# Two-layer hybrid decoder trunk in split float32: buffers of weight parts, rounds of the down projection, and the way of the 32x32 blocks

## The chip, the cores and the metric

The kernel runs on one core of one Trainium2 chip. The metric is the device time of one execution in microseconds (us), lower is better. Before the change three runs gave 2683.37, 2684.74 and 2685.12 us; the median is 2684.74 us. A further execution was profiled: it took 2684.28 us, of which the profile's span covers 2682.6 us.

## What is computed

Input x is 256 tokens by 2048 channels in float32. Two layers follow each other; each is, cut to what matters:

```
h = rms_norm(x); q, k, v, uv, gates = split(h @ w_in)         # 2048 -> 7680
a = sliding_window_attention(rope(norm(q)), rope(norm(k)), v, sinks) @ w_attn_branch
b = chunked_sgu(gelu(uv)) @ w_sgu_branch
x = x + (sigmoid(gates_a) * a + sigmoid(gates_b) * b) @ w_out  # 2048 -> 2048
h2 = rms_norm(x)
x = x + (silu(h2 @ w_gate) * (h2 @ w_up)) @ w_down             # 2048 -> 5632 -> 2048
```

All weights are float32 in HBM, some 235 MB a layer, and each is read once.

## The kernel before

**Three products for one.** A float32 product is made from three matmuls in a rounded 32-bit format: every weight tile is split into a high part `whi` (ScalarE, L199) and the remainder `wlo` (VectorE, L200), every activation unit into `uh` and `ul`; `add_product` (L274 to L283) adds uh by whi, uh by wlo and ul by whi for two blocks of 128 rows. Activations are the stationary operand (128 x 128), weights the moving one (128 x 512).

**Entries.** The work of TensorE is one list of entries. An entry is one weight tile of 256 rows by 512 columns (a raw tile, 512 KB): tags X, G and U stand for a tile that is multiplied with both token blocks (12 matmuls of 512 columns). `single` makes a product of one column chunk. `pair` handles two column chunks (gate and up of the feed-forward, or two chunks of w_out or w_down) and computes the first 512 rows of them by a seven-product scheme in place of eight: tags P1, P2, P6, P7, P4, P5, P3, each 6 matmuls. These need sums of raw tiles (`sums`, L192 on VectorE), taken in place in four tiles k11, k12, k21, k22 that have one buffer each. P6 reads k11 after k12 := k22 - k12 and k11 := k11 + k12; P4 and P5 each need one more sum. After P1, P6 and P7 ScalarE copies a PSUM bank away (`snap`, L307); after P5 VectorE adds one bank to a copy (L309).

**Order.** The body of a pair is G, P5, G, P3, then G and U entries. Where one product ends and a pair begins, the last four entries of the former (t0 to t3 below) are woven between the pair's head: t0, P1, P2, t1, P6, t2, P7, t3, P4. In `pair` a constant TAIL = 6 says how many U entries stand at the end; for w_down, whose pairs have 8 or 10 G and U entries each, the earlier ones alternate.

**Stream.** At every step `Stream.next` asks for loads up to W_LOAD = 5 entries from the current one, splits up to W_SPLIT = 3 entries, the sums of an entry standing right before its split, and hands out the parts. So at the step of entry n the parts of entry n + 2 are issued. There are 3 buffers of `hi` and of `lo` (pool `wsp`), 4 of raw tiles (`wraw`, tag raw) and 28 slots of 4 KB a partition (`big`) for activations. All loads are issued from the SP queue, which is in order.

**Steps.** Other work is put off with `after(n, fn)`: it is run n ticks later, a tick being one entry of 12 matmuls or two of 6. Within an engine this work is placed behind the split that was issued last (`issue_after`). The order of TensorE is that of the program; on the other engines a planner at build time sets the order.

**Turning.** Activations that were computed as tokens by channels must be turned before they can be a stationary operand. `turn` (L342) transposes 32x32 blocks on VectorE into `box` (L349), the second token block a tick later, and 16 small DMAs of 32 KB (L353, SP queue) carry the blocks to the right partitions in `tt` within the next ticks. `transposed` then makes `uh` and `ul` (6 and 7 ticks after the call; for the chunk that the seven-product scheme uses 6 to 9 ticks). With `on_pe` TensorE transposes instead (L391).

**Feed-forward.** `hidden` computes one chunk of 512 of the 5632 hidden channels (eleven in all); the down projection runs in two rounds, after chunks 0 to 4 and after 5 to 10 (ROUNDS). Each round takes two pairs (columns in four chunks) and adds its result to x (`residual`, L805).

Of the kernel before, what the change touches and what calls it, by code (L numbers as in the profile page):

```python
# [8 lines left out]
F32 = mybir.dt.float32  # L9
F32R = mybir.dt.float32r  # L10
AF = mybir.ActivationFunctionType
ALU = mybir.AluOpType
AX = mybir.AxisListType

P = 128
NT = 2
# [11 lines left out]
CW = 512  # L28
NCH = D // CW
EPS = 1e-6  # L30
B = 32
W_LOAD = 5
ROUNDS = ((0, 5), (5, 11))
WINO = 0
TAIL = 6
W_SPLIT = 3
N_WARM = 8
TT = 1
K_TURN = 7
# [11 lines left out]
def hybrid_trunk(ctx: ExitStack, tc: tile.TileContext, x, mix_norm, w_in, q_norm, k_norm, sinks,  # L51
# [3 lines left out]

    const = ctx.enter_context(tc.tile_pool(name="const", bufs=1))
    lay = ctx.enter_context(tc.tile_pool(name="lay", bufs=1))
    big = ctx.enter_context(tc.tile_pool(name="big", bufs=28))
    wraw = ctx.enter_context(tc.tile_pool(name="wraw", bufs=4))
    wsp = ctx.enter_context(tc.tile_pool(name="wsp", bufs=3))  # L60
    tmp = ctx.enter_context(tc.tile_pool(name="tmp", bufs=5))
    turned = ctx.enter_context(tc.tile_pool(name="turned", bufs=TT))
    small = ctx.enter_context(tc.tile_pool(name="small", bufs=4))
    ps_acc = ctx.enter_context(tc.tile_pool(name="ps_acc", bufs=4, space=bass.MemoryType.PSUM))
# [5 lines left out]
    def nm(s):  # L70
        names[0] += 1
        return f"{s}_{names[0]}"
# [41 lines left out]

        return Plan(key, [], [half(w, h, "X") for h in range(w.shape[0] // (2 * P))])

    def pair(key, wa, wb):

        h1, h2 = 2 * WINO, 2 * WINO + 1
        l11, l12, l21, l22 = (load_of(w, h, t) for w, h, t in ((wa, h1, "k11"), (wb, h1, "k12"), (wa, h2, "k21"),
                                                              (wb, h2, "k22")))
        k11, k12, k21, k22 = l11[0], l12[0], l21[0], l22[0]
        rest = [h for h in range(wa.shape[0] // (2 * P)) if h // 2 != WINO]
        g, u = [half(wa, h, "G") for h in rest], [half(wb, h, "U") for h in rest]
        head = [dict(tag="P1", loads=[l11], src=k11), dict(tag="P2", loads=[l21], src=k21),
                dict(tag="P6", loads=[l12, l22], sums=[(k12, k22, "-", k12), (k11, k11, "+", k12)], src=k11),
                dict(tag="P7", loads=[], src=k12), dict(tag="P4", loads=[], sums=[(k21, k21, "-", k11)], src=k21)]
        p5 = dict(tag="P5", loads=[], sums=[(k11, k22, "-", k11)], src=k11)  # L130
        p3 = dict(tag="P3", loads=[], src=k22)
        body = [g[0], p5, g[1], p3]
        n_mid = len(u) - TAIL
        for i, e in enumerate(g[2:]):
            body.append(e)
            if i < n_mid:
                body.append(u[i])
        body += u[min(n_mid, len(g) - 2):]
        return Plan(key, head, body)

    plans = []
    for l in range(DEPTH):
        wl = w_in[l]
        for kind, c in FIRST_PART:
            o = {"kv": O_KV, "q": 0, "v": O_V, "u": O_U, "gate": O_GATE}[kind] + c * CW
            plans.append(single(("in", l), wl[:, o:o + CW]))
        plans += [single(("att", l), w) for w in cols_of(w_attn_branch[l], NCH)]
        for j in range(NCH):
            plans.append(single(("in", l), wl[:, O_GATE + D + j * CW:O_GATE + D + (j + 1) * CW]))
            plans.append(single(("sgu", l), w_sgu_branch[l, :, j * CW:(j + 1) * CW]))  # L150
        c_ = cols_of(w_out[l], NCH)
        plans += [pair(("mix", l), c_[j], c_[j + 1]) for j in range(0, NCH, 2)]
        for r, (f0, f1) in enumerate(ROUNDS):
            for f in range(f0, f1):
                plans.append(pair(("ffn", l), w_gate[l, :, f * CW:(f + 1) * CW], w_up[l, :, f * CW:(f + 1) * CW]))
            c_ = cols_of(w_down[l, f0 * CW:f1 * CW, :], NCH)
            plans += [pair(("hid", l, r), c_[j], c_[j + 1]) for j in range(0, NCH, 2)]
    entries = []
    for p in plans:
        if p.head:  # L160
# [5 lines left out]
    class Stream:  # L166
# [2 lines left out]

        def __init__(self):  # L170
            self.raws, self.parts = {}, []
            self.asked = self.at = 0

        def load(self, upto):
            while self.asked < min(upto, len(entries)):
# [8 lines left out]
                    self.raws[key] = raw  # L184
                self.asked += 1

        def split(self, upto):
            while len(self.parts) < min(upto, len(entries)):
                e = entries[len(self.parts)]
                for d, x, op, y in e.get("sums", ()):  # L190
                    with tc.issue_after(self.last.ins):
                        self.last = nc.vector.tensor_tensor(out=self.raws[d], in0=self.raws[x], in1=self.raws[y],  # L192
                                                            op=ALU.add if op == "+" else ALU.subtract)
                raw = self.raws[e["src"]]
                hi = wsp.tile([P, 2, CW], F32R, tag="hi", name=nm("whi"))
                lo = wsp.tile([P, 2, CW], F32R, tag="lo", name=nm("wlo"))
                one = len(self.parts) < 2
                for i in ([slice(0, 1), slice(1, 2)] if one else [slice(0, 2)]):
                    nc.scalar.activation(hi[:, i, :], raw[:, i, :], AF.Copy)  # L199
                    self.last = nc.vector.tensor_tensor(out=lo[:, i, :], in0=raw[:, i, :], in1=hi[:, i, :].bitcast(F32),  # L200
                                            op=ALU.subtract)
                self.parts.append((hi, lo))

        def next(self):
            self.load(self.at + W_LOAD)
            self.split(self.at + W_SPLIT)
            self.at += 1
            return self.parts[self.at - 1]

# [6 lines left out]
    def after(n, fn):  # L216
        steps.append((slot_no[0] + n, fn))
# [41 lines left out]

    units_at = {}  # L260
    turn_of = [0]
    debt = [0]

    def block(units, h, t):

# [2 lines left out]

    def banks(p, which):
        if which not in p.acc:  # L270
            p.acc[which] = [ps_acc.tile([P, CW], F32, tag="acc", name=nm("acc")) for _ in range(NT)]
        return p.acc[which]

    def add_product(p, ps, u, w):  # L274
# [64 lines left out]
        while p.left:  # L339
            step()  # L340

    def turn(dst, src, per=1):  # L342


        box = turned.tile([P, 4, 4, NT, B], F32, tag="box", name=nm("box"))
        iv = src.rearrange("p t (k j c) -> p t k j c", j=4, c=B)

        def blocks(t):
            nc.vector.transpose(box[:, :, :, t, :].rearrange("p j k r -> p k j r"), iv[:, t])  # L349

        def move(j):
            for i in range(4):
                nc.sync.dma_start(dst[j * B:(j + 1) * B, i], box[i * B:(i + 1) * B, j])  # L353

        blocks(0)
        after(1, lambda: blocks(1))
        for j in range(4):
            after(1 + j // per, lambda j=j: move(j))

    def transposed(units, c, src, cols=None, on_pe=False, wino=False):  # L360

# [37 lines left out]
        def blocks_of(k0):  # L399
            return lambda k, step: tt[:, :, k0 + k:k0 + k + step].rearrange("p i k t r -> p (k t) i r")  # L400

        if not wino:
            def done():
                parts(2, 2, blocks_of(2))
                units[c] = (uh, ul)

            after(6, lambda: parts(0, 2, blocks_of(0)))
            after(7, done)
            return

        flat = {}
# [24 lines left out]
            split_(sh, sl, flat["s"])  # L436
            units[c] = (uh, ul, sh, sl)

        after(6, lambda: scaled(0))
        after(7, lambda: scaled(2))  # L440
        after(8, sums)
        after(9, finished)

    class Norm:

# [144 lines left out]
    class Attention:  # L590
# [46 lines left out]
        def keys(self, kv):  # L637
            self.kv = kv
            kd = slot([P, NT, NKV, 2, HD], name="kd")
            self.rotate(kv[:, :, :KVW], NKV, self.pl.rope[1], [kd[:, :, :, j, :] for j in range(2)])  # L640
            self.kT = slot([P, 4, NKV, NT, B], name="kT")
            after(K_TURN, lambda: turn(self.kT, kd.rearrange("p t n a d -> p t (n a d)"), 2))

        def queries(self, c, q):
            self.rotate(q, NQ // 2, self.pl.rope[0], None)
# [10 lines left out]
        def turn_queries(self, c, q):  # L656
            tt = slot([P, 4, 4, NT, B], name="tt")

            def ordered(k):
                nc.scalar.activation(self.qT[c][:, k:k + 2].rearrange("p k (t i r) -> p (k t) i r", t=NT, r=B),  # L660
                                     tt[:, :, k:k + 2].rearrange("p i k t r -> p (k t) i r"), AF.Copy)

            turn(tt, q, 2)
            after(4, lambda: ordered(0))
            after(5, lambda: ordered(2))

# [155 lines left out]
    for l in range(DEPTH):  # L822
# [44 lines left out]
        if l + 1 < DEPTH:  # L867
            after(20, lambda: prepare(l + 1))

        def hidden(hT, c, wino):  # L870
            hid = slot([P, NT, CW], name="hid")

            def added(sums):
# [12 lines left out]
            def on_up(sums):  # L886
                up = added(sums)
                for t in range(NT):
                    nc.vector.scalar_tensor_tensor(out=hid[:, t, :], in0=up[t], scalar=norm.rr[t], in1=hid[:, t, :],  # L889
                                                   op0=ALU.mult, op1=ALU.mult)  # L890
                after(2, lambda: transposed(hT, c, hid, wino=wino))

            product_pair(("ffn", l), on_gate, on_up)

        for r, (f0, f1) in enumerate(ROUNDS):
            hT = units_at["hid", l, r] = [None] * (f1 - f0)
            for f in range(f0, f1):
                hidden(hT, f - f0, f - f0 == WINO)
            if f1 < NF:
                residual(("hid", l, r))  # L900
            elif l + 1 < DEPTH:
# [42 lines left out]
```

## Time and profile before

| | |
|---|---|
| median of 3 runs | 2684.74 us (2683.37 to 2685.12) |
| profiled execution | 2684.28 us, span 2682.6 us |
| full matmuls (512 columns) | 3 x 3516 |
| DMA traffic | 506.20 MB, mean 189 GB/s |
| w_out, w_gate, w_up, w_down loads | 64, 176, 176, 176 of 512 KB |

Times are us unless marked ns. PE is TensorE's matmul, PEld its weight load, DVE VectorE, ACT ScalarE, POOL GpSimd, SP the queue that issues the DMAs. Matmuls are pipelined: the recorded duration of one is longer than the distance to the next. In the rows of waits, "who <- whom: total, times, longest" is the idle time of an engine before an instruction and what ended it. In groups of instructions the number after x is the count, then busy us and mean ns of one, then the idle time before them.

### The profile page before, as it was taken

Reading aid. Unit: us, or ns where it says so; the run is one execution under the profiler, and the core shown is the slowest. Engines: PE = TensorE matmul, PEld = TensorE weight load, DVE = VectorE, ACT = ScalarE, POOL = GpSimd, SP = SyncE. Lnnn points to the kernel's source line nnn. Section 1 sums busy time; section 2 is a strip of 40 time slices with the busy share of each in tenths; the row PEclk is TensorE's granted clock in tenths of the full one; section 3 lists DMA queues with packets and bytes.
Section 4 is the critical chain, followed back from the end, with each engine's and each line's share of the span. In section 5 each row is a group of like instructions: output and inputs, shape, how many; then the busy total and the mean of one; then the engine's idle time right before and its main releaser. Section 6 shows DMA issues by size and latency. Waiting matters only on the chain.

```text
span 2682.6 us, 30911 instructions
## 1 busy us (share of the span) xinstructions
PE 2550.2 (95%) x11102; PEld 2032.9 (76%) x11102; DVE 1859.6 (69%) x2229; ACT 1305.8 (49%) x1626; POOL 43.2 (2%) x47
## 2 busy tenths in 40 slices
PE   9999999998999999999999999999999999999999
PEld 7788887776777777777787888877767777767777
DVE  6686556777776667776667865667776776776765
ACT  5455444554444445444545554445554544454443
POOL 2000000000000000000000000000000000000000
PEclk9999999999999999999999999999999999999999
DMA  7655666654665665565666556665556556556555
GB/s 245 217 149 170 208 202 187 195 189 150 192 200 177 192 194 176 178 204 193 202 195 215 165 176 187 215 189 187 174 183 193 185 185 203 171 180 202 176 190 157
DMA packets 288715, 506.20 MB, mean 189 GB/s; under 512 B 28016, under 2 KB 56784, under 8 KB 288560
## 3 DMA queue, kind: packets, MB, share of 16 engines
q1 hardware_dynamic: 287888, 503.69, 60.3%
q8 instruction: 87, 1.43, 0.2%
q0 software_dynamic: 352, 0.25, 0.1%
q14 instruction: 68, 0.56, 0.1%
q10 hardware_dynamic: 320, 0.27, 0.0%
HBM read 475.27 MB, written 2.10 MB: 178 GB/s over the span
## 4 chain that ended last, share of the span: by engine, by line
PE 59%; DVE 18%; ACT 7%; DMA 6%; SPq 5%; issue 4%; POOL 0%; ACTq 0%; DVEq 0%
PE acc L282 20%; PE acc L283 19%; PE acc L281 18%; DVE wlo L200 9%; ACT whi L199 6%; SPq L353 5%; DVE raw L192 4%; DMA raw<-in_w_up_dram 2%; DMA raw<-in_w_in_dram 1%; DVE snap L876 1%; DMA raw<-in_w_down_dram 1%; DVE box L349 1%; PE po L715 1%; DVE hid L889 1%; DMA tt<-box 1%
## 5 line engine op out<-in xcount | busy, mean ns | idle before, releaser
L200 DVE TENSOR_TENSOR wlo<-raw,whi 128x1024 fp32r<-128x1024 f32 (+1 forms) x1000 | 1207.8, 1219 | 725.9 <-ACT whi L199 716.9
L199 ACT ACTIVATE whi<-raw 128x1024 fp32r<-128x1024 f32 (+1 forms) x1000 | 1037.0, 1055 | 1179.9 <-PE acc L283 686.8
L282 PE MATMUL acc<-wlo,uh 128*128 128x512 f32 x3244 | 1282.0, 395 | 36.6 <-DVE wlo L200 33.0
L281 PE MATMUL acc<-whi,uh 128*128 128x512 f32 x3244 | 1275.0, 393 | 9.6 <-ACT whi L199 8.4
L283 PE MATMUL acc<-whi,ul 128*128 128x512 f32 x3244 | 1268.1, 391 | 0.0
L282 PEld LDWEIGHTS acc<-wlo,uh 128*128 128x128 f32 x3244 | 611.8, 189 | 209.8 <-DVE wlo L200 86.3
L281 PEld LDWEIGHTS acc<-whi,uh 128*128 128x128 f32 x3244 | 611.9, 189 | 142.3 <-ACT whi L199 12.8
L283 PEld LDWEIGHTS acc<-whi,ul 128*128 128x128 f32 x3244 | 611.9, 189 | 124.6 <-DVE ul L382 0.2
L192 DVE TENSOR_TENSOR raw<-raw,raw 128x1024 f32<-128x1024 f32 x136 | 165.8, 1219 | 0.6
L282 PE MATMUL acc<-wlo,sh 128*128 128x512 f32 x272 | 114.0, 419 | 48.4 <-DVE wlo L200 48.4
L281 PE MATMUL acc<-whi,sh 128*128 128x512 f32 x272 | 113.0, 416 | 29.3 <-ACT whi L199 27.3
L282 PEld LDWEIGHTS acc<-wlo,sh 128*128 128x128 f32 x272 | 51.1, 188 | 79.2 <-DVE wlo L200 70.8
L307 ACT ACTIVATE snap<-acc 128x512 f32<-128x512 f32 x102 | 60.9, 597 | 100.4 <-PE acc L283 100.4
L283 PE MATMUL acc<-whi,sl 128*128 128x512 f32 x272 | 107.1, 394 | 0.0
L281 PEld LDWEIGHTS acc<-whi,sh 128*128 128x128 f32 x272 | 51.1, 188 | 62.0 <-ACT whi L199 53.2
L876 DVE TENSOR_TENSOR snap<-acc,snap 128x512 f32<-128x512 f32 x66 | 45.3, 687 | 31.7 <-PE acc L283 31.5
L283 PEld LDWEIGHTS acc<-whi,sl 128*128 128x128 f32 x272 | 51.3, 189 | 8.4
L374 DVE TENSOR_TENSOR ul<-tt,uh 128x512 fp32r<-128x512 f32 x60 | 41.1, 685 | 0.0
L805 DVE SCALAR_TENSOR_TENSOR xs<-acc,xs 128x512 f32<-128x512 f32 (+1 forms) x50 | 31.9, 663 | 9.6 <-PE acc L283 9.6
L373 ACT ACTIVATE uh<-tt 128x512 fp32r<-128x512 f32 x60 | 34.1, 617 | 3.9 <-DMA tt<-box 3.9
L889 DVE SCALAR_TENSOR_TENSOR hid<-snap,rr,hid 128x512 f32<-128x512 f32 x44 | 32.8, 745 | 0.0
L258 POOL TENSOR_TENSOR rstd<-var,neg_half 128x1 f32<-128x1 f32 x8 | 7.1, 894 | 1534.7 <-DVE var L467 1534.7
(130 smaller groups left out, 824.7 us busy)
## 6 DMA issues: line engine op xcount, KB each, us to landing
raw<-in_w_in_dram SPq DMA_DIRECT2D x239, 512.0 KB, 4.4
raw<-in_w_up_dram SPq DMA_DIRECT2D x176, 512.0 KB, 4.6
raw<-in_w_gate_dram SPq DMA_DIRECT2D x176, 512.0 KB, 3.8
raw<-in_w_down_dram SPq DMA_DIRECT2D x176, 512.0 KB, 4.3
raw<-in_w_out_dram SPq DMA_DIRECT2D x64, 512.0 KB, 4.5
tt<-box SPq DMA_DIRECT2D x784, 32.0 KB, 2.6
raw<-in_w_attn_branch_dram SPq DMA_DIRECT2D x32, 512.0 KB, 4.3
raw<-in_w_sgu_branch_dram SPq DMA_DIRECT2D x32, 512.0 KB, 4.7
```

The costliest lines, as they stand in the source:

```text
L192: self.last = nc.vector.tensor_tensor(out=self.raws[d], in0=self.raws[x], in1=self.raws[y], op=ALU.add if op == "+" else ALU.subtract)
L199: nc.scalar.activation(hi[:, i, :], raw[:, i, :], AF.Copy)
L200: self.last = nc.vector.tensor_tensor(out=lo[:, i, :], in0=raw[:, i, :], in1=hi[:, i, :].bitcast(F32), op=ALU.subtract)
L281: nc.tensor.matmul(ps, a, hi[:, kk, :], start=first and kk == 0, stop=False, skip_group_check=True)
L282: nc.tensor.matmul(ps, a, lo[:, kk, :], start=False, stop=False, skip_group_check=True)
L283: nc.tensor.matmul(ps, b, hi[:, kk, :], start=False, stop=kk == 1, skip_group_check=True)
L307: nc.scalar.activation(p.snaps[tag], a[1], AF.Copy)
L353: nc.sync.dma_start(dst[j * B:(j + 1) * B, i], box[i * B:(i + 1) * B, j])
L373: nc.scalar.activation(h, s_, AF.Copy)
L374: nc.vector.tensor_tensor(out=l, in0=s_, in1=h.bitcast(F32), op=ALU.subtract)
L876: nc.vector.tensor_tensor(out=x[1], in0=x[0], in1=x[1], op=ALU.add)
L889: nc.vector.scalar_tensor_tensor(out=hid[:, t, :], in0=up[t], scalar=norm.rr[t], in1=hid[:, t, :], op0=ALU.mult, op1=ALU.mult)
```

## The change

It has five parts.

1. **Buffers and lead.** `wsp` has 4 buffers in place of 3 and W_SPLIT is 4; `wraw` has 5 in place of 4 and W_LOAD is 7; `big` has 25 slots in place of 28. At the step of entry n the parts of entry n + 3 are issued.
2. **Sums.** The sums of raw tiles are issued by a routine of their own, for entries up to n + 5 at step n (W_SUM = 6), behind the split of entry n + 3. The loads of the four k tiles belong to P1 and P2.
3. **Rounds.** The down projection runs in three rounds of 4, 4 and 3 chunks. Each round has two pairs, so there are two more pairs in a layer. The first pair of a round (`late`) puts the last two G and the last two U entries at its end; all others have G entries, then U entries. With three chunks the last one is transposed on TensorE.
4. **PSUM.** The first accumulators of every second pair come from the pool `ps_at` (two banks) and not from `ps_acc`.
5. **Turning.** `box` goes to a DRAM tile `far` in one DMA of 512 KB, and four DMAs of 128 KB each bring the blocks back to `tt`. All five are issued a tick after the call, together with the second token block. The units that wait for `tt` are made a tick sooner (5 and 6 ticks after the call).

```
-W_LOAD = 5
-ROUNDS = ((0, 5), (5, 11))
+W_LOAD = 7
+ROUNDS = ((0, 4), (4, 8), (8, 11))
-TAIL = 6
-W_SPLIT = 3
+TAIL = 2
+W_SPLIT = 4
+W_SUM = 6
...
-    big = ctx.enter_context(tc.tile_pool(name="big", bufs=28))
-    wraw = ctx.enter_context(tc.tile_pool(name="wraw", bufs=4))
-    wsp = ctx.enter_context(tc.tile_pool(name="wsp", bufs=3))
+    big = ctx.enter_context(tc.tile_pool(name="big", bufs=25))
+    wraw = ctx.enter_context(tc.tile_pool(name="wraw", bufs=5))
+    wsp = ctx.enter_context(tc.tile_pool(name="wsp", bufs=4))
+    dram = ctx.enter_context(tc.tile_pool(name="dram", bufs=2, space=bass.MemoryType.DRAM))
...
+        head = [dict(tag="P1", loads=[l11, l12], src=k11), dict(tag="P2", loads=[l21, l22], src=k21),
+                dict(tag="P6", loads=[], sums=[(k12, k22, "-", k12), (k11, k11, "+", k12)], src=k11),
...
+        body = [g[0], p5, g[1], p3] + g[2:-2] + u[:-TAIL] + g[-2:] + u[-TAIL:] if late else \
+            [g[0], p5, g[1], p3] + g[2:] + u
...
+        def add(self, upto):
+            while self.summed < min(upto, len(entries)):
+                for d, x, op, y in entries[self.summed].get("sums", ()):
+                    with tc.issue_after(self.last.ins):
+                        self.last = nc.vector.tensor_tensor(out=self.raws[d], in0=self.raws[x], in1=self.raws[y],
+                                                            op=ALU.add if op == "+" else ALU.subtract)
+                self.summed += 1
...
             self.split(self.at + W_SPLIT)
+            self.add(self.at + W_SUM)
...
+            if p.paired and which == "a":
+                odd[0] = not odd[0]
+            pool, tag = (ps_at, "at") if p.paired and which == "a" and odd[0] else (ps_acc, "acc")
...
-        def move(j):
-            for i in range(4):
-                nc.sync.dma_start(dst[j * B:(j + 1) * B, i], box[i * B:(i + 1) * B, j])
+        far = dram.tile([P, 4, 4 * NT * B], F32, tag="far", name=nm("far"))
+
+        def gather():
+            nc.sync.dma_start(far, box.rearrange("p j k t r -> p j (k t r)"))
+            for j in range(4):
+                nc.sync.dma_start(dst[j * B:(j + 1) * B].rearrange("c i k t r -> c i (k t r)"),
+                                  far[:, j].rearrange("(i c) x -> c i x", c=B))
...
-            after(6, lambda: parts(0, 2, blocks_of(0)))
-            after(7, done)
+            after(5, lambda: parts(0, 2, blocks_of(0)))
+            after(6, done)
...
-                after(2, lambda: transposed(hT, c, hid, wino=wino))
+                after(2, lambda: transposed(hT, c, hid, on_pe=c == len(hT) - 1 == 2, wino=c == WINO))
```

More of the change, by code (lines that the diff above doesn't have):

```diff
@@ L115, in single, with pair @@
         return Plan(key, [], [half(w, h, "X") for h in range(w.shape[0] // (2 * P))])
-    def pair(key, wa, wb):
+    def pair(key, wa, wb, late=False):
         h1, h2 = 2 * WINO, 2 * WINO + 1
@@ L126, in pair @@
         g, u = [half(wa, h, "G") for h in rest], [half(wb, h, "U") for h in rest]
-        head = [dict(tag="P1", loads=[l11], src=k11), dict(tag="P2", loads=[l21], src=k21),
-                dict(tag="P6", loads=[l12, l22], sums=[(k12, k22, "-", k12), (k11, k11, "+", k12)], src=k11),
+        head = [dict(tag="P1", loads=[l11, l12], src=k11), dict(tag="P2", loads=[l21, l22], src=k21),
+                dict(tag="P6", loads=[], sums=[(k12, k22, "-", k12), (k11, k11, "+", k12)], src=k11),
                 dict(tag="P7", loads=[], src=k12), dict(tag="P4", loads=[], sums=[(k21, k21, "-", k11)], src=k21)]
@@ L131, in pair @@
         p3 = dict(tag="P3", loads=[], src=k22)
[L132 to L138, printed above, removed]
+        body = [g[0], p5, g[1], p3] + g[2:-2] + u[:-TAIL] + g[-2:] + u[-TAIL:] if late else \
+            [g[0], p5, g[1], p3] + g[2:] + u
         return Plan(key, head, body)
@@ L156, in hybrid_trunk @@
             c_ = cols_of(w_down[l, f0 * CW:f1 * CW, :], NCH)
-            plans += [pair(("hid", l, r), c_[j], c_[j + 1]) for j in range(0, NCH, 2)]
+            plans += [pair(("hid", l, r), c_[j], c_[j + 1], j == 0) for j in range(0, NCH, 2)]
     entries = []
@@ L171, in __init__ @@
             self.raws, self.parts = {}, []
-            self.asked = self.at = 0
+            self.asked = self.summed = self.at = 0
         def load(self, upto):
@@ L189, in split @@
                 e = entries[len(self.parts)]
[L190 to L193, printed above, removed]
                 raw = self.raws[e["src"]]
@@ L261, in hybrid_trunk @@
     turn_of = [0]
-    debt = [0]
+    debt, odd = [0], [False]
     def block(units, h, t):
@@ L270, in banks @@
         if which not in p.acc:
-            p.acc[which] = [ps_acc.tile([P, CW], F32, tag="acc", name=nm("acc")) for _ in range(NT)]
+            if p.paired and which == "a":
+                odd[0] = not odd[0]
+            pool, tag = (ps_at, "at") if p.paired and which == "a" and odd[0] else (ps_acc, "acc")
+            p.acc[which] = [pool.tile([P, CW], F32, tag=tag, name=nm("acc")) for _ in range(NT)]
         return p.acc[which]
@@ L340, in product_pair, with turn @@
             step()
-    def turn(dst, src, per=1):
+    def turn(dst, src):
         box = turned.tile([P, 4, 4, NT, B], F32, tag="box", name=nm("box"))
@@ L349, in blocks @@
             nc.vector.transpose(box[:, :, :, t, :].rearrange("p j k r -> p k j r"), iv[:, t])
-        def move(j):
-            for i in range(4):
-                nc.sync.dma_start(dst[j * B:(j + 1) * B, i], box[i * B:(i + 1) * B, j])
+        far = dram.tile([P, 4, 4 * NT * B], F32, tag="far", name=nm("far"))
[4 more added lines that the diff above has]
+                                  far[:, j].rearrange("(i c) x -> c i x", c=B))
         blocks(0)
-        after(1, lambda: blocks(1))
-        for j in range(4):
-            after(1 + j // per, lambda j=j: move(j))
+        after(1, lambda: (blocks(1), gather()))
     def transposed(units, c, src, cols=None, on_pe=False, wino=False):
@@ L437, in finished @@
             units[c] = (uh, ul, sh, sl)
[L439 to L442, printed above, removed]
+        after(5, lambda: scaled(0))
+        after(6, lambda: scaled(2))
+        after(7, sums)
+        after(8, finished)
     class Norm:
@@ L641, in keys @@
             self.kT = slot([P, 4, NKV, NT, B], name="kT")
-            after(K_TURN, lambda: turn(self.kT, kd.rearrange("p t n a d -> p t (n a d)"), 2))
+            after(K_TURN, lambda: turn(self.kT, kd.rearrange("p t n a d -> p t (n a d)")))
         def queries(self, c, q):
@@ L661, in ordered @@
                                      tt[:, :, k:k + 2].rearrange("p i k t r -> p (k t) i r"), AF.Copy)
-            turn(tt, q, 2)
+            turn(tt, q)
             after(4, lambda: ordered(0))
@@ L868, in hybrid_trunk, with hidden @@
             after(20, lambda: prepare(l + 1))
-        def hidden(hT, c, wino):
+        def hidden(hT, c):
             hid = slot([P, NT, CW], name="hid")
@@ L897, in hybrid_trunk @@
             for f in range(f0, f1):
-                hidden(hT, f - f0, f - f0 == WINO)
+                hidden(hT, f - f0)
             if f1 < NF:
```

## The prediction, made before the change was run

> **What bounds the kernel now.** I read the page's busy times first, then stretches of the span by stage, then the waits of each engine, then the timeline around one pair.
>
> ```profile
> span 2682.6 us, 30911 instructions
> PE 2550.2 (95%) x11102; PEld 2032.9 (76%) x11102; DVE 1859.6 (69%) x2229; ACT 1305.8 (49%) x1626; POOL 43.2 (2%) x47
> ```
>
> By its busy row PE has 132 us to lose. The stretches say more: count, not busy time, shows the pace.
>
> ```profile
> 459.10:1350.70 891.60, 832.21 (x3503) 652.00 (x3502) 636.73 (x696) 436.18 (x509) 2.08 (x2) 0.99 0.59 186
> 1790.80:2668.60 877.80, 821.42 (x3460) 645.13 (x3459) 621.93 (x653) 425.94 (x486) 1.08 (x2) 0.99 0.59 185
> 1624.60:1790.80 166.20, 166.20 (x734) 137.30 (x733) 98.81 (x103) 77.10 (x84) 0.00 (x0) 1.00 0.68 210
> 525.00:600.00 75.00, 66.83 (x274) 51.94 (x273) 55.54 (x83) 39.13 (x54) 2.08 (x2) 0.95 0.60 187
> ```
>
> The third row has single products only: 166.20 / 734 = 0.2264 us a matmul, with DMA at 210 GB/s. The first two rows hold all pairs of the two layers (w_out, gate/up, w_down): 891.60 - 3503 x 0.2264 = 98.5 us and 877.80 - 3460 x 0.2264 = 94.5 us are lost. So 193 us is the ceiling of what the pairs can give back, not 132. The Trainium skill (Perfetto Trace Analysis, "Identifying the Most-Contended Engine") calls matmul busy time a poor measure of headroom, since matmuls are pipelined; by that rule the ceiling of 132 is not to be used, and the trace agrees. The fourth row is the start of a stage (w_out into the first gate/up pairs); it loses 13 of its 75 us.
>
> ```profile
> PE acc L282 <- DVE wlo L200: 81.4, 134, 1.9
> PE acc L281 <- ACT whi L199: 35.7, 44, 2.0
> PE pt L391 <- DVE gate L860: 3.0, 1, 3.0
> ACT whi L199 <- PE acc L283: 686.8, 444, 5.7
> ACT whi L199 <- DVE raw L192: 225.0, 66, 4.3
> ACT whi L199 <- DMA raw<-in_w_up_dram: 84.4, 27, 5.7
> ACT whi L199 <- DMA raw<-in_w_down_dram: 37.2, 23, 5.1
> ```
>
> PE waits for weight parts and hardly anything else. ACT, which makes the first part, waits for PE to free a buffer (444 times) and for the sums of raw tiles (66 times, two a pair for 34 pairs less two): the parts are made just in time. Here is the head of one pair:
>
> ```profile
> 609.81 1.23 DVE L200 TENSOR_TENSOR wlo<-raw,whi 128x1024 fp32r<-128x1024 f32 x1 [1.45 <-ACT whi L199]
> 610.95 2.48 DVE L192 TENSOR_TENSOR raw<-raw,raw 128x1024 f32<-128x1024 f32 x2
> 614.61 3.50 DVE L200 TENSOR_TENSOR wlo<-raw,whi 128x1024 fp32r<-128x1024 f32 x3 [1.18 <-ACT whi L199]
> 613.52 2.96 ACT L199 ACTIVATE whi<-raw 128x1024 fp32r<-128x1024 f32 x3 [2.85 <-DVE raw L192]
> 613.73 0.39 PE L283 MATMUL acc<-whi,ul 128*128 128x512 f32 x1
> 614.63 0.51 PE L281 MATMUL acc<-whi,sh 128*128 128x512 f32 x1 [0.52 <-ACT whi L199]
> 615.89 0.50 PE L282 MATMUL acc<-wlo,sh 128*128 128x512 f32 x1 [0.75 <-DVE wlo L200]
> 622.80 0.69 DVE L876 TENSOR_TENSOR snap<-acc,snap 128x512 f32<-128x512 f32 x1 [1.50 <-PE acc L283]
> ```
>
> The chain before P6 is two sums, then whi, then wlo. PE comes to P6 at 613.73 + 0.23 and starts it at 614.63; the second matmul follows after 1.26 in place of 0.23. These two stops cost 0.67 and 1.03 us, while their recorded idle is 0.52 and 0.75: each wait costs some 0.21 us more than the row says, so the 178 waits are worth 81.4 + 35.7 + 178 x 0.21 = 155 us.
>
> **Four buffers, sums sooner.** Durations: whi 1.05 us (L199), wlo and a sum 1.14 us from start to start on DVE (609.81 to 610.95), a snap 0.6, as these rows have them:
>
> ```profile
> L199 ACT ACTIVATE whi<-raw 128x1024 fp32r<-128x1024 f32 (+1 forms) x1000 | 1037.0, 1055 | 1179.9 <-PE acc L283 686.8
> L307 ACT ACTIVATE snap<-acc 128x512 f32<-128x512 f32 x102 | 60.9, 597 | 100.4 <-PE acc L283 100.4
> L805 DVE SCALAR_TENSOR_TENSOR xs<-acc,xs 128x512 f32<-128x512 f32 (+1 forms) x50 | 31.9, 663 | 9.6 <-PE acc L283 9.6
> L391 PE MATMUL pt<-ident,xs 128*128 128x128 f32 x56 | 7.7, 275 | 0.3 <-DVE xs L805 0.2
> L431 DVE TENSOR_TENSOR sums<-flat 128x256 f32<-128x256 f32 x16 | 6.0, 419 | 0.0
> ```
>
> Put zero at the start of t0 and let PE run at full pace: 2.72 us for t, G and U (12 matmuls), 1.36 for a P. It then wants P6 at 8.15, t2 at 9.5, P7 at 12.2, t3 at 13.6, P4 at 16.3, G0 at 17.7, P5 at 20.4, G1 at 21.7, P3 at 24.5.
>
> With three buffers the parts of entry n + 2 may be written once n - 1 is done. P2 starts at 4.08; then DVE still has wlo of t1 until 5.0, two sums until 7.3, whi until 8.35, wlo until 9.5: P6's second matmul, due at 8.4, is about 1.1 us late. The trace says 1.03, so the method holds.
>
> With four buffers the parts of n + 3 are written once n - 1 is done, and the sums stand two steps further ahead. Going through the two queues in order (snaps in ACT's, and on DVE after t3 the four up operations of 0.66 each), wlo is ready for P6 at 5.0, t2 6.9, P7 8.0, t3 10.4, P4 12.3, G0 14.5, P5 16.4, G1 20.2, P3 21.3. The margins are 3.2, 2.6, 4.2, 3.2, 4.0, 3.2, 4.0, 1.5 and 3.2 us: none is late. Without the sooner sums P6 would be ready at 6.7, still in time, so the fourth buffer does most. On DVE the moved sums stand ahead of the two splits that they followed; their 2.3 us are in the times above. The lead hides 13 splits and the sums; if DVE falls more than 1.5 us behind, G1 is late first.
>
> I let the 155 us go, less 12 for the starts of stages, where PE waits for activations (the fourth stretch loses 13 us of 75, against some 8 at the average 193 / 1769 of the pairs, and such starts come at mix and at gate/up in each layer; the 3.0 us wait for a gate is one). That leaves a gain of 143. The other 38 of the 193 us are delays too short to appear as waits; kept, with zero as their other end.
>
> **Loads.** W_LOAD costs and brings nothing by itself: SP waits for buffers (1552.5 us), not to be asked. The four k tiles have buffers of their own and come long before. A raw tile's load waits until the tile 4 (then 5) before it is split:
>
> ```profile
> SPq L180 <- DVE wlo L200: 1552.5, 647, 7.7
> 632.34 0.37 SPq L180 DMA_DIRECT2D raw<-in_w_gate_dram  x1
> 633.01 8.26 SPq L353 DMA_DIRECT2D tt<-box  x12
> 641.38 0.53 SPq L180 DMA_DIRECT2D raw<-in_w_up_dram  x1
> 641.95 2.41 SPq L353 DMA_DIRECT2D tt<-box  x4
> DMA to landing us min/median/max: 3.5/4.3/11.1
> raw<-in_w_up_dram SPq DMA_DIRECT2D x176, 512.0 KB, 4.6
> tt<-box SPq DMA_DIRECT2D x784, 32.0 KB, 2.6
> out_dram<-xs SPq DMA_DIRECT2D x6, 256.0 KB, 4.2
> ```
>
> Slack before: tile r - 4 is split at entry r - 6 plus 2.3 us (whi, wlo), tile r is wanted at r - 2, four entries or 10.9 us; less 2.3 and 4.3 of landing there remain 4.3 us. A turn puts 16 issues (8.26 + 2.41 = 10.7 us, 0.67 each) before the next loads: too long, and the up tiles come late. After: five entries, 13.6 - 2.3 - 4.3 = 7.0 us. Those waits are among the 155.
>
> **The turn.** Five issues are 3.3 us. The four reads must wait for `far` to land, and on SP whatever stands behind them waits too: raw loads, if the planner has not put them between. `far` is not in the trace. Bounds: 2.6 us (32 KB) and 11.1 us (the slowest raw tile); I take 4.5, by the 512 KB loads (4.3) and the 256 KB stores (4.2). Worst block 4.5 + 4 x 0.67 = 7.2 us against 7.0 of slack and at least 1.5 of margin: nothing. From `box` to `tt` it is 7.2 + some 3.5 for the last read, 10.7 us against 9.5 us (G1, P3, G2, G3) until ACT comes to `uh`; the 1.2 us are within the margins (0, else 49 x 1.2 = 59 if these are used up). Traffic grows by 49 x 0.52 MB, to 530 MB or 208 GB/s at the predicted time; the third stretch ran at 210 without loss.
>
> **Three rounds.** Four more pairs in all. Each saves one product of eight, 6 matmuls: -24 x 0.2264 = -5.4 us. Two last chunks turned on PE: 16 transposes at 7.7 / 56 = 0.14, +2.2 us, and PE then waits for `hid`: t3's end plus P4 and G0 (4.1 us) against up operations interleaved with splits (4 to 6 us), 0 to 2 us each, +3 with the drain. On DVE: two residuals of 14 operations at 0.66, 12 splits and 16 sums at 1.14, two more first chunks (four operations of 0.42 and a split): some 56 us, hence 1916 / 2545 = 75% busy. In the short pairs (31.3 us of PE) DVE has 19 x 1.14 + 7 x 0.66 + 0.6 = 27 us: covered, else 0 to 1 us each. With `ps_at` a pair's second accumulators use the banks of the pair before in half of the cases; a residual frees them 3 to 5 us after t3, wanted at 4.1: 0 to 1 us in eight pairs. I put +4 for both. The 25 slots: I count from the code 10 for the normalized rows, 10 for a round of four, and 4 passing ones; no wait.
>
> **The sum.** 2684.3 (profiled run; the median is 2684.7) - 143 - 5.4 + 2.2 + 3 + 4 = 2545 us.
>
> **The rivals.**
> *Half stays.* DVE is in order, and operations that wait for PE stand in its queue (1.50 us idle at 622.80). If they hold up wlo of G1 and of what follows, the last three stops of a head stay and half of the 143 returns: 2545 + 72 = 2617. Against it: a 1.5 us margin in the tightest place.
> *The round trip blocks SP: slower.* A stall begins when `far` takes over 7.0 + 2.7 - 2.7 = 7.0 us (slack, usual margin, the four issues). Over that each us costs 49 us; from 9.8 us the 139 us gained are gone; at 11.1 us it is 2545 + 201 = 2746. For it: the largest landing, and the planner may leave nothing between. Against it: medians of 4.2 and 4.3 for like transfers, and that 10.7 us of issues cost little now. The Trainium skill (DMA: Bandwidth & Descriptors, "Anatomy of one DMA") warns that the write receipt is most of a DMA's fixed time and heaviest with HBM as target. By its fit, 2.0 us and bytes over 436 GB/s, `far` would take 3.2 us, an estimate from that page (its fit is of another issue path); no run here shows it.
> *25 slots are too few.* With 24 of 25 used, a write waits for a reader on PE; 1 to 3 us in the 16 gate/up pairs of the rounds of four: +32, 2577. Against it: that count is reached only in a round's last pairs.
> *No effect.* If late loads were the true cause of the waits, faster pairs would only wait longer: 2684 - 5 = 2679. Against it: 444 waits for a buffer against some 50 for tiles of w_up and w_down.
>
> **How the numbers follow.** Forecast 0.70, half stays 0.14, slots 0.08, no effect 0.03, slower 0.05. The range reaches from 2505 (the 38 small us gone too, 2507) to 2620 (half stays). A difference within 0.2%, 5.4 us, is about what a measurement of this kernel can't tell from none. Faster 0.92, same 0.03, slower 0.05.
>
> **What would show it.** Right: the wait of PE for wlo falls from 81.4 to under 20 us, for whi from 35.7 to under 10; ACT no longer waits for L192; each pair's stretch comes near 0.2264 us a matmul; 10524 full matmuls; `far` lands within 6 us. Wrong: PE's waits for parts stay above 60 us, or SP shows long waits for `far` and ACT waits for raw tiles.

## The result and the profile after

The changed kernel takes 2531.7 us (median of 4 runs, 2530.42 to 2534.11) against 2684.93 us on the same chip: a ratio of 0.9431, 95% interval 0.9415 to 0.9447. The forecast was 2545 us. The profiled execution has a span of 2528.7 us. The page's busy times:

```profile
span 2528.7 us, 30348 instructions
PE 2480.7 (98%) x11094; PEld 2043.9 (81%) x11094; DVE 1906.9 (75%) x2293; ACT 1334.7 (53%) x1658; POOL 43.8 (2%) x47
```

The same stretches as in the prediction, where they now lie: the pairs of layer 0 and of layer 1, the single products between, four pairs in a row (two of the down projection and two of gate/up), and the stretch in which the second gate/up pair of the first round ends and the third begins. The columns are the stretch and its length, the busy time and count of each engine, then PE's granted clock, DMA share and GB/s.

```profile
453.00:1265.70 812.70, 795.80 (x3500) 656.18 (x3498) 653.70 (x716) 448.19 (x519) 2.08 (x2) 1.00 0.66 213
1706.40:2516.50 810.10, 792.57 (x3464) 652.02 (x3463) 646.48 (x685) 441.98 (x502) 1.08 (x2) 0.99 0.64 207
1540.50:1706.40 165.90, 165.90 (x734) 137.37 (x733) 99.61 (x104) 76.83 (x84) 0.00 (x0) 1.00 0.66 213
975.00:1145.00 170.00, 170.00 (x752) 140.76 (x751) 132.58 (x135) 91.23 (x99) 0.00 (x0) 1.00 0.65 211
610.00:642.00 32.00, 27.51 (x115) 22.26 (x114) 23.77 (x42) 16.38 (x21) 0.00 (x0) 0.95 0.53 173
```

The pace of the single products is as before, 165.90 / 734 = 0.2260 us a matmul. At that pace the pairs lose 812.70 - 3500 x 0.2260 = 21.7 us and 810.10 - 3464 x 0.2260 = 27.2 us, together 49 us in place of 193. That is 144 of the 154 us by which the span fell; 5.4 us of the rest are the 24 matmuls fewer. In the fourth row, with four heads in it, nothing is lost: 170.00 / 752 = 0.2261. In the last row 6 of 32 us are lost, so what is left sits in few places. PE's waits name it:

```profile
PE acc L287 <- ACT snap L313: 26.7, 9, 4.5
PE pt L399 <- DVE xs L813: 4.5, 3, 2.8
PE acc L289 <- DVE ul L390: 3.9, 2, 3.4
PE acc L288 <- DVE wlo L202: 2.7, 7, 0.6
PE pt L399 <- DVE hid L897: 2.6, 2, 2.0
```

The wait for wlo is 2.7 us (81.4 before), that for whi is gone from the list (35.7 before). A wait that did not stand in the list before is the longest: nine times PE waits for a snap, ACT's copy of a PSUM bank. ACT's own waits show what became of the other causes:

```profile
ACT whi L201 <- PE acc L289: 682.6, 504, 3.5
ACT uh L381 <- DMA tt<-far: 77.4, 22, 5.8
ACT whi L201 <- DVE raw L189: 65.4, 22, 6.1
ACT flat L426 <- DMA tt<-far: 33.8, 9, 5.5
ACT whi L201 <- DMA raw<-in_w_gate_dram: 6.6, 4, 1.7
ACT whi L201 <- DMA raw<-in_w_down_dram: 3.4, 1, 3.4
```

Late raw tiles are gone (84.4 and 37.2 us before for w_up and w_down). Waiting for PE to free a buffer goes on, 504 times, but PE hardly feels it now: the parts are made a whole entry earlier than before. ACT also still waits for sums (65.4 us in 22 waits; 225.0 in 66 before). And the turned tile is late: with two more rows (18.4 and 12.1 us) ACT waits 142 us for `tt`. On SP a turn looks like this, with the waits of the reads and the landings behind it:

```profile
600.99 2.76 SPq L178 DMA_DIRECT2D raw<-in_w_up_dram  x2
604.01 0.34 SPq L360 DMA_DIRECT2D far<-box  x1
605.12 2.10 SPq L178 DMA_DIRECT2D raw<-in_w_up_dram  x2
610.37 2.99 SPq L362 DMA_DIRECT2D tt<-far  x4
```

```profile
SPq L362 <- DMA far<-box: 139.9, 49, 5.5
```

```profile
far<-box SPq DMA_DIRECT2D x49, 512.0 KB, 6.0
tt<-far SPq DMA_DIRECT2D x188, 128.0 KB, 3.4
```

The planner puts two raw loads between the write and the reads. SP still stands for 139.9 / 49 = 2.9 us a turn.

### The profile page after: what moved, and what is told of

Same layout as the page of the kernel before. It is cut to its first block, busy times and chain, and to the rows that moved or that the text cites. A ratio compares the mean times of both kernels' runs of the same rounds, so it can differ in the third digit from the quotient of the medians.

```text
span 2528.7 us, 30348 instructions
## 1 busy us (share of the span) xinstructions
PE 2480.7 (98%) x11094; PEld 2043.9 (81%) x11094; DVE 1906.9 (75%) x2293; ACT 1334.7 (53%) x1658; POOL 43.8 (2%) x47
## 4 chain that ended last, share of the span: by engine, by line
PE 91%; DVE 3%; DMA 3%; ACT 2%; issue 1%; SPq 0%; DVEq 0%; ACTq 0%
PE acc L287 29%; PE acc L289 29%; PE acc L288 29%; DVE wlo L202 2%; ACT whi L201 1%; PE po L723 1%; DMA far<-box 1%; DMA raw<-in_w_in_dram 1%; PE psc L684 1%; PE ppt L713 0%; DMA raw<-in_w_gate_dram 0%; DVE raw L189 0%; DMA tt<-far 0%; PE pt L399 0%; DVE xs L813 0%
## 5 line engine op out<-in xcount | busy, mean ns | idle before, releaser
L202 DVE TENSOR_TENSOR wlo<-raw,whi 128x1024 fp32r<-128x1024 f32 (+1 forms) x1012 | 1227.7, 1220 | 506.9 <-ACT whi L201 487.6
L201 ACT ACTIVATE whi<-raw 128x1024 fp32r<-128x1024 f32 (+1 forms) x1012 | 1059.9, 1056 | 924.2 <-PE acc L289 682.6
L287 PE MATMUL acc<-whi,uh 128*128 128x512 f32 x3204 | 1257.2, 392 | 0.8 <-ACT uh L385 0.5
L289 PE MATMUL acc<-whi,ul 128*128 128x512 f32 x3204 | 1250.1, 390 | 3.9 <-DVE ul L390 3.9
L288 PE MATMUL acc<-wlo,uh 128*128 128x512 f32 x3204 | 1251.1, 390 | 2.7 <-DVE wlo L202 2.7
L289 PEld LDWEIGHTS acc<-whi,ul 128*128 128x128 f32 x3204 | 603.6, 188 | 131.4 <-DVE ul L390 4.8
L189 DVE TENSOR_TENSOR raw<-raw,raw 128x1024 f32<-128x1024 f32 x152 | 185.5, 1220 | 1.0
L289 PE MATMUL acc<-whi,sl 128*128 128x512 f32 x304 | 120.1, 395 | 0.0
L813 DVE SCALAR_TENSOR_TENSOR xs<-acc,xs 128x512 f32<-128x512 f32 (+1 forms) x66 | 42.7, 668 | 9.2 <-PE acc L289 9.2
L813 DVE SCALAR_TENSOR_TENSOR xs<-snap,xs 128x512 f32<-128x512 f32 (+1 forms) x50 | 33.0, 663 | 0.0
```

The lines of the kernel that those rows point to most:

```text
L287: nc.tensor.matmul(ps, a, hi[:, kk, :], start=first and kk == 0, stop=False, skip_group_check=True)
L288: nc.tensor.matmul(ps, a, lo[:, kk, :], start=False, stop=False, skip_group_check=True)
L289: nc.tensor.matmul(ps, b, hi[:, kk, :], start=False, stop=kk == 1, skip_group_check=True)
L813: nc.vector.scalar_tensor_tensor(out=xs[:, t, sl], in0=part[:, i * w:(i + 1) * w], scalar=scale, in1=xs[:, t, sl], op0=ALU.mult, op1=ALU.add)
```

## The experiments

Two theories were at odds first: that parts are made too late for want of a buffer (the prediction's), and that other things make them late: the chain over the sums alone, DVE's queue, or late raw tiles. The first four runs do one part of the change alone on the kernel before.

**The fourth buffer alone.**

```
-W_SPLIT = 3
+W_SPLIT = 4
...
-    big = ctx.enter_context(tc.tile_pool(name="big", bufs=28))
+    big = ctx.enter_context(tc.tile_pool(name="big", bufs=26))
...
-    wsp = ctx.enter_context(tc.tile_pool(name="wsp", bufs=3))
+    wsp = ctx.enter_context(tc.tile_pool(name="wsp", bufs=4))
```

> The kernel before with the fourth buffer of weight parts and W_SPLIT = 4 alone (26 slots in place of 28; sums still right before their split). Theory A (parts are made too late for want of a buffer): the working of the pair's head has every part ready in time with four buffers, with or without sooner sums, so most of the 155 us of PE's waits go and those caused by late raw tiles (some 25 us) stay: 2565 us, between 2550 and 2590; PE's waits for wlo fall from 81.4 to under 30 us. Theory B (operations that wait for PE hold up DVE's queue): half stays, 2610 us. Theory C (late raw tiles are the cause): no change, 2680 us.

Measured: 2596.12 us against 2688.69, ratio 0.966 (0.9641 to 0.9678), a gain of 92 us, between theory A and B. The waits of PE, then of ACT and DVE:

```profile
PE acc L282 <- DVE wlo L200: 37.1, 68, 0.8
PE acc L281 <- ACT snap L307: 14.2, 3, 5.0
PE acc L281 <- ACT whi L199: 11.4, 16, 2.3
```

```profile
ACT whi L199 <- DVE raw L192: 194.4, 89, 5.9
ACT whi L199 <- DMA raw<-in_w_up_dram: 95.6, 35, 9.9
ACT whi L199 <- DMA raw<-in_w_down_dram: 77.1, 43, 9.0
DVE snap L876 <- PE acc L283: 94.7, 18, 7.2
```

Half of PE's waits stay (62.7 us in these rows, 117.1 before). Two causes stand in the rows, and no run parts them. ACT waits longer for raw tiles than before (95.6 and 77.1 us against 84.4 and 37.2) and still for sums, so the tiles do not arrive for the buffer more. And DVE waits 94.7 us for PE with the addition of L876, where it waited 31.5 us before, which is theory B's cause.

**Sooner sums alone.**

```
+W_SUM = 5
...
             self.split(self.at + W_SPLIT)
+            self.add(self.at + W_SUM)
```

> The kernel before with the sums of raw tiles issued two entries sooner and nothing else (three buffers of parts, the four k tiles loaded with P1 and P2). Theory A: the two stops before and in P6 (1.8 us a pair, 34 pairs) and a part of those at P4 to P5 go, 62 to 110 us: 2600 us. If the chain over sums is the only cause, all of it goes and the fourth buffer adds nothing: 2550 us. Theory C: 2680 us.

Measured: 2593.29 us, ratio 0.9651 (0.9633 to 0.9668), a gain of 94 us, inside theory A's 62 to 110. PE's waits:

```profile
PE acc L288 <- DVE wlo L205: 46.2, 88, 2.2
PE acc L287 <- ACT whi L204: 10.8, 9, 2.2
```

So either part alone takes away some 60% of the 153 us that the whole change brings. Their sum is more than the whole, so they are in part two ways to the same microseconds, and neither is the sole cause.

**Three rounds alone.**

```
-ROUNDS = ((0, 5), (5, 11))
+ROUNDS = ((0, 4), (4, 8), (8, 11))
```

(The edit also has the pairs' order, the alternating banks and the last chunk's turn on PE.)

> The kernel before with three rounds of the down projection alone, with the order of their pairs, the alternating banks and the last chunk's turn on TensorE that belong to them; three buffers, late sums and the old turn stay. Theory A: 24 matmuls fewer are 5.4 us, but four more heads with stops of some 5 us each are 20 us, and the turns on PE are 5 us: slower by 20 us, 2704 us. If the stops are not per head: 2680 us.

Measured: 2716.38 us, ratio 1.0106 (1.0091 to 1.0121), slower by 28 us. The 24 matmuls are saved, but PE's waits for parts grow to 130.5 us from 117.1 with the four heads more. The theory of heads at the old price gave 20 us; what the rest is was not taken apart. That the part pays behind the others was not run: no run takes it out of the changed kernel.

**The turn alone.**

> The kernel before with the turn through DRAM alone (5 DMAs, the waiting units a tick sooner). If 16 issues on SP are what makes the tiles of w_up and w_down late: the waits of ACT for them (84.4 and 37.2 us) fall to under 30 us and PE gains 15 to 25 us, 2665 us. If the round trip is the worse delay: ACT waits 50 us or more for the turned tile and the kernel is slower by 10 to 40 us, 2705 us.

The edit is part 5 of the change. Measured: 2681.87 us, ratio 0.9973 (0.9957 to 0.9988), 7 us less. ACT's waits say why both theories were half right:

```profile
ACT uh L376 <- DMA tt<-far: 95.8, 26, 5.4
ACT flat L421 <- DMA tt<-far: 27.2, 6, 6.1
ACT whi L200 <- DMA raw<-in_w_up_dram: 7.4, 4, 2.7
ACT whi L200 <- DMA raw<-in_w_down_dram: 5.5, 5, 2.0
```

The raw tiles come in time (7.4 and 5.5 us of waiting), and ACT waits for the turned tile in their place. One delay is exchanged for another, and PE gains little: its waits for parts are 112.6 us against 117.1.

The next four take one part out of the changed kernel.

**Three buffers of parts.** `W_SPLIT = 3`, `W_SUM = 5`, `wsp` with 3 buffers, `big` with 27 slots.

> The changed kernel with three buffers of parts (W_SPLIT 3, sums still two entries sooner, 27 slots). With sums alone the kernel before gained 95 us and kept 63 us of PE's waits. If the fourth buffer is needed for what is left: 2580 us, PE's waits for parts 40 us or more. If sooner sums, the turn and five raw tiles do it without the fourth buffer: 2540 us.

Measured: 2577.04 us, ratio to before 0.9589 (0.9574 to 0.9603), against 0.9431 for the whole change: the fourth buffer is worth 42 us (0.0158 x 2688) beside the sooner sums. PE's waits for parts are 51.4 us again.

**Late sums.** The sums stand right before their split; four buffers stay.

> The changed kernel with the sums right before their split again; four buffers stay. By the working of the pair's head P6 is then ready at 6.7 us and wanted at 8.15: no loss, 2532 us, and the sums are worth nothing beside four buffers. If they stand behind other work in DVE's and ACT's queues, as four buffers alone showed (194 us of ACT's waits for sums, 66 us of PE's waits left): slower by 30 to 50 us, 2570 us.

Measured: 2539.71 us, ratio 0.9444 (0.9427 to 0.9461). Against the changed kernel's 0.9431 that is 0 to 8 us. PE's waits for parts:

```profile
PE acc L288 <- DVE wlo L203: 14.1, 28, 1.3
PE acc L287 <- ACT whi L202: 7.0, 4, 3.9
```

The net is small, as the working of the head had it (6.7 against 8.15 us), but not because every part is in time: PE waits 21.1 us for parts, where the changed kernel has 2.7. In exchange the waits for the snap, 26.7 us in the changed kernel, are gone. In the third gate/up pair of the first round, for one, ACT makes the snap of P1 before P6's `whi` here, and after it in the changed kernel. So the sooner sums take away one wait and bring another. What they are worth without the other was not run.

**The old turn.** `turn` and the ticks as before.

> The changed kernel with the old turn (16 DMAs from box, units at the old ticks); all else stays. If the turn through DRAM is a gain because it frees SP: raw tiles come late again (7.0 us of slack against 10.7 us of issues) and the kernel is slower by 10 to 25 us, 2550 us. If its late landing (ACT waits 142 us for it in the changed kernel, 25 us before) costs more than SP's freedom brings: ACT's waits for tt fall under 40 us, the stops of 4 to 5 us in the second pair of each round go, and it is faster by 10 to 30 us, 2515 us.

Measured: 2526.15 us, ratio 0.9401 (0.9387 to 0.9415): not slower, rather 6 us faster. ACT waits 35.7 us for tiles of w_up and 32 us for `tt`, and PE waits for the snap 21.0 us. So SP's freedom is no longer needed; that the fifth raw tile carries the 10.7 us of issues is likely, but no run has the changed kernel with four. And the stops at the snap are not from the late turned tile, or they would have gone: in the six places where they are longest the recorded waits sum to 20.9 us here and to 22.9 in the changed kernel.

**Units a tick later.** The units are made at the old ticks, the turn stays.

> The changed kernel with the units that wait for the turned tile at the old ticks (6, 7, 8, 9 in place of 5 to 8). If ACT's wait for the turned tile blocks its queue and so the snap that P6 waits for: ACT's waits for tt fall from 142 us to under 70 us, PE's waits for the snap from 26.7 to under 12 us, 2515 us. If those stops come from DVE's backlog in the round's first chunk (its sums, ul, sl) and not from the late tile: 2530 us, no change. If the later units come too late for the pairs that need them, PE waits for uh or ul: slower, 2540 us.

Measured: 2534.45 us, ratio 0.9432 (0.9411 to 0.9452): no change. PE's waits for the snap are 25.2 us. By itself this run says little on the late tile, since ACT still waits 112 us for `tt` and not under 70; the run with the old turn says more. What causes the stops is in the timeline of the changed kernel, where the second gate/up pair of a round ends and the head of the third is woven in. DVE, ACT, then PE:

```profile
624.43 0.76 DVE L439 TENSOR_TENSOR sums<-flat 128x256 f32<-128x256 f32 x2
626.24 1.22 DVE L189 TENSOR_TENSOR raw<-raw,raw 128x1024 f32<-128x1024 f32 x1
...
629.84 1.23 DVE L189 TENSOR_TENSOR raw<-raw,raw 128x1024 f32<-128x1024 f32 x1
630.97 0.43 DVE L439 TENSOR_TENSOR sums<-flat,sums 128x256 f32<-128x256 f32 x1
...
632.27 3.50 DVE L202 TENSOR_TENSOR wlo<-raw,whi 128x1024 fp32r<-128x1024 f32 x3
```

```profile
624.00 1.06 ACT L201 ACTIVATE whi<-raw 128x1024 fp32r<-128x1024 f32 x1 [0.28 <-ACT whi L201]
631.18 2.95 ACT L201 ACTIVATE whi<-raw 128x1024 fp32r<-128x1024 f32 x3 [6.12 <-DVE raw L189]
634.04 1.04 ACT L430 ACTIVATE sh<-sums 128x1024 fp32r<-128x1024 f32 x1
634.98 1.04 ACT L201 ACTIVATE whi<-raw 128x1024 fp32r<-128x1024 f32 x1
635.93 0.57 ACT L313 ACTIVATE snap<-acc 128x512 f32<-128x512 f32 x1
```

```profile
631.68 0.39 PE L289 MATMUL acc<-whi,ul 128*128 128x512 f32 x1
636.55 0.50 PE L287 MATMUL acc<-whi,sh 128*128 128x512 f32 x1 [4.49 <-ACT snap L313]
```

P6 adds to the bank that the snap of P1 must have copied. DVE makes the first chunk's own sums and splits in the midst of the head, so the second sum of raw tiles ends at 631.07. ACT stands idle for 6.12 us for it, and in its queue four whi and the split `sh` come before the snap, which ends at 636.50. PE starts P6 at 636.55, 4.64 us late. P6's own parts were late too, but by less: its whi ends at 632.2 and its wlo at 633.5, at most 1.4 us behind their time. Another operation in ACT's queue came last. At this place DVE also prepares small tables for the next layer, 1.0 us just before the second sum. The five other stops of this kind (3.55 to 3.94 us late by the starts of the matmuls) have the same order in both queues without the tables, and ACT stands idle for 5.0 to 5.5 us in each.

**That work moved past the head.** The second half of making a round's first chunk, 12 ticks later:

```
-        after(7, sums)
-        after(8, finished)
+        after(7 + wait, sums)
+        after(8 + wait, finished)
...
-                after(2, lambda: transposed(hT, c, hid, on_pe=c == len(hT) - 1 == 2, wino=c == WINO))
+                after(2, lambda: transposed(hT, c, hid, on_pe=c == len(hT) - 1 == 2, wino=c == WINO, wait=12))
```

> The changed kernel; in the feed-forward alone the second half of making a round's first chunk (its split, the sums for the seven-product scheme and their split) 12 ticks later, past the next pair's head. Theory: the stops of 4 to 5 us in the second pair of each round (six places, some 33 us with their followers) come from that work on DVE and ACT: it stands ahead of the raw tiles' sums, ACT waits for those with the split for P6, and the snap of P1, which P6 needs, stands behind. Then PE's waits for the snap fall from 26.7 to under 6 us: 2505 us, between 2498 and 2512. Rival: the late turned tile is the cause; then nothing changes, 2530 us.

Measured: 2494.55 us against 2681.22, ratio 0.9303 (0.929 to 0.9317). The changed kernel on the same chip:

> The changed kernel itself once more, on the same chip as the three others, for their comparison: 2532 us.

Measured: 2530.9 us, ratio 0.9438 (0.9424 to 0.9452). The move is worth 36 us, more than the 27 expected, and the time lies below the expected 2498 to 2512. PE's longest waits and the stretch from 610 to 642 us are now:

```profile
PE pt L399 <- DVE xs L813: 4.3, 3, 2.7
PE acc L289 <- DVE ul L390: 3.9, 2, 3.4
PE pt L399 <- DVE hid L897: 2.3, 2, 2.0
PE acc L287 <- ACT snap L313: 2.2, 2, 1.8
```

```profile
610.00:642.00 32.00, 32.00 (x143) 26.50 (x142) 26.31 (x43) 18.94 (x24) 0.00 (x0) 1.00 0.63 206
```

143 matmuls where there were 115, at full clock. The 36 us can be followed in the trace of the run that it is compared with, by the starts of the matmuls: there the six stops hold P6 up by 24.4 us in all, and in the 15 us behind each stop the matmuls lie 11.1 us in all further apart than at 0.2265 us, together 35.5. The late turned tile still costs ACT about what it did (73.4 and 32.1 us in its two largest rows), and of PE's waits only one of 0.6 us, for `uh`, can come from it.

**The same with the old turn, and the old turn again.**

> As d2_spread with the old turn of 16 DMAs. If the turn through DRAM is worth nothing here either, it is 3 to 8 us under d2_spread, as the changed kernel with the old turn was under the changed kernel: 2500 us. If both differ by less than 0.2%, the turn is of no weight.

Measured: 2496.26 us, ratio 0.9307 (0.9294 to 0.932): equal to the run with the DRAM turn within 0.1%.

> The changed kernel with the old turn once more, on the chip of the run below: 2526 us; under the changed kernel by 5 us if the first look was right, equal to it if that was the chip.

Measured: 2525.01 us, ratio 0.9413 (0.9399 to 0.9427), 6 us under the changed kernel as in the first run of it. So the turn through DRAM has a small price as long as the first chunk's work crowds the head, and none without.

## Why the prediction was right, point by point

**The ceiling of 193 us, not 132.** Right: 144 us came back in the pairs alone, more than the 132 us that PE's busy row left.

**155 us of waits go, 12 stay: a gain of 143.** The pairs' loss fell by 144, but the two numbers agree partly by chance. The sum kept 12 + 38 = 50 us of loss in the pairs and 49 are measured, but they are not the same ones. The waits for parts went almost wholly (2.7 us left). The 38 us of small delays, which the sum kept, went for the most part too: the six stops at the snap take 23.9 us of the 49, by the starts of the matmuls, and the slower matmuls behind them 11.2 us, so at most 14 us are left for all else. Those stops no step had foreseen.

**"None is late" in the working of the head.** It nearly held for wlo and whi and fell short for the snap. The head was worked out for a pair without a first chunk's work in it, and for the parts alone; the snap was in ACT's queue as a duration and not as something that PE waits for. In six pairs of 38 it was the last to come (22.9 of the 26.7 us), and there the move of that work, which changes no part's buffer, gave 36 us. So two terms were mis-sized, in opposite directions: 12 us for the remaining waits, placed at the starts of stages rather than at the head of the third gate/up pair of a round, and 38 us for small delays.

**The fourth buffer does most.** Shown in the changed kernel: without it 42 us are lost, without the sooner sums 0 to 8. But "still in time" without them was too good (21.1 us of waits for parts); the net is small because the waits for the snap go at the same time. Alone, on the kernel before, the two give the same (92 and 94 us).

**Loads.** Right for the changed kernel: ACT's waits for raw tiles are nearly gone. By the same working (7.0 us of slack) the old turn's 10.7 us of issues would make tiles late with five raw tiles too. They do, ACT waits 35.7 us for those of w_up, but it costs no time.

**The turn at nothing.** The net was right and the terms were off: `far` lands after 6.0 us (4.5 taken), ACT waits 142 us for `tt`, and it costs no time once the head is clear; in the changed kernel as it stands the turn costs some 6 us. The rival of a blocked SP had `far` over 7.0 us as its condition. The largest landing of `far` was 9.4 us, but with loads put between SP stood for 5.5 us at the longest (the row of its waits).

**Three rounds: -5.4 us and small costs.** 24 matmuls fewer, as counted. The turns on PE wait 2.6 us for `hid`, taken as 3 with their drain. That the part costs time without the others was not said: alone it is slower by 28 us.

**DVE at 75% and 208 GB/s.** Measured 75% (1906.9 of 2528.7 us) and 210 GB/s; neither bound.

**The signs.** The waits for wlo and whi fell as said, and there are 10524 full matmuls. Two signs did not come: ACT still waits 65.4 us for sums, and `far` lands within 6 us only in the median.

What stays open: no run takes the fifth raw tile, the alternating banks, the pairs' order, the 25 slots or the three rounds alone out of the changed kernel, and none has the late sums together with the first chunk's work moved.

## What to carry to other kernels

Count an engine's instructions over a stretch against its best pace: here the busy row hid a third of the loss. When parts arrive just in time, work the queue of the engine that makes them through one repeat of the pattern, and put into it everything that the bound engine waits for, copies out of PSUM too, not the operand alone. A part of a change may cost time by itself, as the three rounds do here, and two parts may pay for the same microseconds; taking each out of the whole shows what it is worth there.

## What the runs showed of the hardware

A stop of PE often costs more than itself. In the stretch around the 4.64 us stop the granted clock is 0.95 over 32 us, 1.6 us at full speed, and in the run without the stop it is 1.00; over the whole span the clock went from 0.994 to 0.998. Behind that stop the matmuls start 0.43 us apart for some 3.4 us, then 0.23 again. The six stops differ, though all are 3.55 to 4.64 us long: by the starts of the matmuls three cost 1.7 to 1.8 us more, two 2.8 to 3.0 and one, of 3.55 us, only 0.14. One of the two dearer ones lies in this stretch:

```profile
1884.00:1916.00 32.00, 28.21 (x112) 22.54 (x110) 26.84 (x28) 15.73 (x17) 0.00 (x0) 0.89 0.53 169
```

The Trainium skill (TensorE: Matmul & The Clock Gate, "Part 1: The HAM clock gate") says that an idle window of some 3.4 us brings the clock to half until a window of that length has been busy. Half of such a window, 1.7 us a stop, is an estimate from that page: the trace agrees for three of the six stops.

A write of 512 KB from SBUF to DRAM landed after 6.0 us in the median, 2.6 to 9.4 us, where loads of that size took 4.2 to 4.9 in the same trace. By the fit of the Trainium skill (DMA: Bandwidth & Descriptors, "Anatomy of one DMA"), which the page gives for the GpSimd issue path, an estimate is 3.2 us; here, issued from SP among the raw loads, it took nearly twice that.
